# Splitting plain weight pieces two ahead instead of one in a Trainium2 macaron layer

## The chip, the cores and the metric

The kernel runs on one core of one Trainium2 chip. A core has engines that run side by side, each with its own queue in program order: TensorE (PE: matmuls into PSUM, and PEld: weight loads), VectorE (DVE), ScalarE (ACT), GpSimd (POOL, not used here) and SyncE (SP), whose queue issues the transfers from the chip's memory (DMA). The metric is device microseconds of one execution; shorter is better. The runs of the kernel before took 1015.99, 1016.55 and 1015.99 us (median 1015.99).

## The reference: what is computed

One layer on 512 tokens of width 1024: a half-weighted SwiGLU feed-forward, a mixer, a second half-weighted feed-forward, each behind an RMS norm and added to the residual, and a last norm.

```python
h = h + 0.5 * swiglu(rmsnorm(h, ffn1_norm[l]), ffn1_w_in[l], ffn1_w_out[l])
h = h + hybrid_mixer(rmsnorm(h, mix_norm[l]), w_mix_in[l], ...)
h = h + 0.5 * swiglu(rmsnorm(h, ffn2_norm[l]), ffn2_w_in[l], ffn2_w_out[l])

def swiglu(x, w_in, w_out):
    gate, up = jnp.split(x @ w_in, 2, axis=-1)
    return (jax.nn.silu(gate) * up) @ w_out
```

A feed-forward is 2816 wide (22 blocks of 128). The mixer projects to queries, keys and values of eight heads with compressed, selected and windowed attention and eight heads with a 128-token window, and ends in one more product, `w_mix_out`. All data are float32.

## The kernel before, in words

**Precision by parts.** TensorE takes the operands in a rounded 32-bit format. To keep float32 accuracy every operand is split: the high part is the rounded copy, the low part the rest, and a product is three matmuls, high x high, low x high, high x low (L207, L208, L209 for 512 tokens; L305, L306, L307 for 256). The normalized input is split once (`parts`, L162 on ACT and L163 on DVE). Weights are split piece by piece in `to_parts`: L97 is the ACT copy that makes the high part, L98 the DVE subtraction that makes the low part.

**The plain stream.** Weights that are used plainly come in pieces of 128 x 1024 in one stream: six pieces for the first three blocks (0, 1, 2) of each feed-forward (a gate piece and an up piece for each block), and the mixer's weights between them. `load_next` issues a piece's transfer, at most NRAW = 4 ahead; `split_next` takes the oldest loaded piece, splits it and loads another; `next_w` hands out the oldest split piece and splits one more, so that one split piece stands ready while one is used. A split piece takes two of the 32 buffers named `u`; a pair of raw pieces takes one of the four `t` buffers.

**A feed-forward's first blocks** (`ffn`, the loop `for j in range(plain)`). Each piece is one product `mm3` of eight contraction blocks, 24 matmuls. Beside them run the norm's sums: L170/L171 squares, `rstd_col` (L184 on PE, L186 and a table load on ACT, L188 on DVE) and `rstd_bc` (L195 on PE, L199 on ACT, into `bc`). Then each block's gated value: `gated` reads the gate product (L332, DVE), takes the silu (L334, ACT, behind a table load), reads the up product (L336), multiplies (L338), and splits the result (L325, L327).

**The side work** (`side_step`). The other 19 blocks use a form with seven products of quarter size in place of eight. It needs sums of the input, `sums_of_x`: eight scaled copies on ACT (L230), then per group differences on DVE (L238, L239, L242, L243) and splits (L246 on ACT, L247 on DVE); and sums of the weights, `sums_of_w`: L273, L277, L283 on DVE and splits (L275/L278, L281/L284, L287/L289, L292/L294). Block 3's first product needs the parts of L275 and L278. L483 sets two PSUM banks ahead of these products.

**The mixer's last product** is `mix_out((2, 3), True)`: two pieces, four output blocks from each; each output is added to the residual (L1077) and fed to the second feed-forward's norm.

**What sets the order.** The program is written in the order of the calls above, and a list scheduler with its own estimate of durations then orders each engine's queue. On the chip an engine takes its queue strictly in that order, and waits only where an instruction needs another engine's result or a free buffer.

Of the kernel before, what the change touches and what calls it, by code (L numbers as in the profile page):

```python
# [44 lines left out]
def tile_hybrid(ctx, tc, xT, f1_wi, f1_wo, wm_t, wm_n, cw1, cw2, small, wm_oa, wm_ob, wm_oc, f2_wi, f2_wo, const, out):  # L45
# [9 lines left out]
    def ps(tag="mm"):  # L55
        return psp.tile([P, 512], F32, tag=tag, name=tag, bufs=NB[tag])
# [4 lines left out]
    def ps_any():  # L61
        turn[0] += 1
        return ps(wide_ps[turn[0] % 5])

    def flat(dt=F32R):
        return sb.tile([P, 1024], dt, tag="u", name="u", bufs=NU)
# [25 lines left out]
    stream = []  # L92
    loaded, split = [], []
    half = []

    def to_parts(raw, wh, wl, c):
        A.copy(wh[:, c], raw[:, c])  # L97
        V.tensor_tensor(wl[:, c], raw[:, c], f(wh[:, c]), op=ALU.subtract)  # L98

    def raw_piece():  # L100
        if not half:
            t = double()
            half.extend([t[:, 0:1024], t[:, 1024:2048]])
        return half.pop(0)

    def load_next():
        if stream:
            src, n, whole = stream.pop(0)
            raw = raw_piece()
            nc.sync.dma_start(raw[:, :n], src)  # L110
            loaded.append((raw, n, whole))

    def split_next():
        if not loaded:
            load_next()
        if loaded:
            raw, n, whole = loaded.pop(0)
            if whole:
                split.append(raw)
            else:  # L120
                wh, wl = flat(), flat()
                to_parts(raw, wh, wl, slice(0, n))
                split.append((wh, wl))
            load_next()

    def load_ahead():
        while len(loaded) < NRAW and stream:
            load_next()

    def next_w():  # L130
        load_ahead()
        if not split:
            split_next()
        w = split.pop(0)
        split_next()
        return w

    def use(*pieces, n=1024, whole=False):
# [26 lines left out]
    def squares(k, acc):  # L165
        if k == 0:
            A.activation(acc, h[:, k, :], AF.Square)
        else:
            sq = tmp()
            A.activation(sq, h[:, k, :], AF.Square)  # L170
            V.tensor_tensor(acc, acc, sq, op=ALU.add)  # L171

    def feed(k, gcol, xs, acc):
        parts(k, gcol, xs)
        squares(k, acc)
# [4 lines left out]
    def rstd_col(acc):  # L180

        pc = ps("pv")
        for t in range(4):
            PE.matmul(pc[:, t : t + 1], acc[:, t * P : (t + 1) * P], ones[:, 0:1], start=True, stop=True)  # L184
        rc = sb.tile([P, 4], F32, tag="rc", name="rc", bufs=2)
        A.activation(rc, pc[:, 0:4], AF.Sqrt, scale=1.0 / D, bias=epsc[:, 0:1])  # L186
        rcol = sb.tile([P, 4], F32, tag="rcol", name="rcol", bufs=2)
        V.reciprocal(rcol, rc)  # L188
        return rcol

    def rstd_bc(rcol):

        pb = ps("pv")
        for t in range(4):
            PE.matmul(  # L195
                pb[:, t * P : (t + 1) * P], rcol[:, t : t + 1].to_broadcast([P, P]), ident, start=True, stop=True
            )
        bc = sb.tile([P, 512], F32, tag="bc", name="bc", bufs=1)
        A.copy(bc, pb)  # L199
        return bc  # L200

    def mm3_steps(o, wh, wl, ks, xs, first, last):
        for q, k in ks:
            c = slice(q * P, (q + 1) * P)
            s0 = first and k == ks[0][1]
            s1 = last and k == ks[-1][1]
            PE.matmul(o, wh[:, c], xs[k][:, 0, :], start=s0, stop=False)  # L207
            PE.matmul(o, wh[:, c], xs[k][:, 1, :], start=False, stop=False)  # L208
            PE.matmul(o, wl[:, c], xs[k][:, 0, :], start=False, stop=s1)  # L209
            yield 0.65  # L210

    def run(gen):
        for _ in gen:
            pass

    def mm3(*a):
        run(mm3_steps(*a))
# [36 lines left out]
    def load_raw(wi, j):  # L254
        t = double()
        for a in range(2):
            nc.sync.dma_start(t[:, a * 1024 : (a + 1) * 1024], wi[j, a])
        return t
# [50 lines left out]
    def ffn(xs, acc, wi, wo, plain, gnext):  # L309
# [20 lines left out]
        def gated(j, pg, pu):  # L330
            z = tmp()
            V.tensor_tensor(z, pg, bc, op=ALU.mult)  # L332
            sg = tmp()
            A.activation(sg, z, AF.Silu)  # L334
            zu = tmp()
            V.tensor_tensor(zu, pu, bc, op=ALU.mult)  # L336
            gg = tmp()
            V.tensor_tensor(gg, zu, sg, op=ALU.mult)  # L338
            run(put_g(j, gg))
# [86 lines left out]
        def side_step(n=1):  # L426
            for _ in range(n):
                while side and next(side[0], side) is side:
                    side.pop(0)
# [3 lines left out]
        for j in range(plain):  # L433
            pz = []
            if state["squares"] and j == 0:

                two = [(split.pop(0), ps_any()) for _ in range(2)]
                pz = [o for _, o in two]
                steps = [mm3_steps(o, wh, wl, ALLK, xs, True, True) for (wh, wl), o in two]
                for _ in ALLK:  # L440
                    for g in steps:
                        next(g, None)
                for g in steps:
                    run(g)
                split_next()
                for _ in range(4):
                    squares(*state["squares"].pop(0))
                side_step(4)
            for s in range(2 - len(pz)):
                wh, wl = next_w()  # L450
                o = ps_any()
                mm3(o, wh, wl, ALLK, xs, True, True)
                pz.append(o)
                if bc is None:
                    todo = state["squares"]
                    for _ in range(4):
                        if todo:
                            squares(*todo.pop(0))
                    if not todo and rcol is None:
                        rcol = rstd_col(acc)  # L460
                    elif rcol is not None:
                        bc = rstd_bc(rcol)
                        while held:
                            gated(*held.pop(0))
                side_step(4)
            if bc is None:
                held.append((j, *pz))
            else:
                gated(j, *pz)
            if j == 0:  # L470
                load_ahead()
                for n in range(2):
                    raws[plain + n] = load_raw(wi, plain + n)
                side.append(sums_of_w(raws, wi, plain, WF))
# [107 lines left out]
    for _ in range(2):  # L582
        src, _n, _whole = stream.pop(0)
        raw, wh, wl = raw_piece(), flat(), flat()
# [30 lines left out]
    for k in range(4, KB):  # L615
        parts(k, S_G1, xs)
    state["squares"] = [(k, acc) for k in range(KB)]
    xs, acc = ffn(xs, acc, f1_wi, f1_wo, NP1, S_GM)


# [38 lines left out]
    def proj(b, o):  # L659
        wh, wl = next_w()  # L660
        yield from mm3_steps(o, wh, wl, ALLK, xs, True, True)
# [29 lines left out]
    def network(kv):  # L691
# [5 lines left out]
        for c in range(2):  # L697
            oc = o[:, c * 64 : c * 64 + 62]
            for mh in range(2):
                w = next_w()  # L700
                for mm in range(8):
                    m = mh * 8 + mm
                    PE.matmul(  # L703
                        oc, w[:, mm * P : (mm + 1) * P], frv[:, mh, :, m : m + 241 : 8], start=m == 0, stop=m == 15
                    )
                    if mm % 4 == 3:
                        yield 0.86
            b1 = sm[:, S_B1 + kv * 2 + c : S_B1 + kv * 2 + c + 1]
            V.tensor_scalar(hT[:, c, :], oc, b1, None, op0=ALU.add)
# [358 lines left out]
    def mix_out(kbs, last):  # L1068
        n = len(kbs)
        per = KB // n  # L1070
        for c in range(KB // per):
            wh, wl = next_w()
            for j in range(per):
                i = c * per + j
                o = ps()
                yield from mm3_steps(o, wh, wl, [(j * n + q, kb) for q, kb in enumerate(kbs)], OB, True, True)
                V.tensor_tensor(h[:, i, :], o, h[:, i, :], op=ALU.add)  # L1077
                if last:
                    feed(i, S_G2, nxs, nacc)
# [78 lines left out]
    piece("q6", queries(6))  # L1158
    piece("q7", queries(7))
    piece("oa", mix_out((4, 5, 6, 7), False), [("s", 0, 3)])  # L1160
    piece("ob", mix_out((0, 1), False), [("n", 0, 3, 2)])
    nxs = []
    nacc = new_acc()
# [13 lines left out]
    while advance() is not None:  # L1177
        pass
    run(mix_out((2, 3), True))


    ffn(nxs, nacc, f2_wi, f2_wo, NP2, None)


# [90 lines left out]
```

## Time and profile before

| | |
|---|---|
| median of the runs | 1015.99 us |
| the profiled execution's own time | 1014.31 us |
| its span, first to last instruction | 1012.5 us |
| mean granted TensorE clock | 0.988 |
| PE busy | 982.1 us (97%) |
| PEld busy | 869.0 us (86%) |
| DVE busy | 804.2 us (79%) |
| ACT busy | 509.6 us (50%) |

A row of a timeline gives start, duration, engine, line, operation, output <- input and the count; in brackets the engine's idle time just before it and what ended it. A row of waits reads: who waited <- for whom: total us, times, longest. A row of windows is explained where it is shown. Granted clock is TensorE's, as a share of full speed. Names of buffers carry no meaning beyond the tile's name: `u` is a split operand, `t` a raw weight buffer, `sc`, `mm` and `pv` are PSUM tiles, `tmp` and `bc` vectors of 512 tokens.

### The profile page before, as it was taken

What the parts mean: (1) busy time and instruction counts of PE and PEld (TensorE: products, weight loads), DVE (VectorE), ACT (ScalarE), POOL (GpSimd) and SP (SyncE); (2) the same over time, 40 slices, a digit from 0 to 9 for tenths busy, and PEclk for the clock granted to TensorE, in tenths of its full rate; (3) what the DMA queues carried; (4) which work ended last, traced back from release to release, by engine and by line L of the source; (5) the groups of instructions that cost most, each with busy time, mean ns of one, the idle gap of its engine ahead of it and who ended that gap; (6) DMA issues with size and microseconds to landing.
All of it is one profiled execution on the core that took longest, in us unless ns stands there. A gap on an engine that the chain in (4) does not pass through costs nothing.

```text
span 1012.5 us, 15908 instructions
## 1 busy us (share of the span) xinstructions
PE 982.1 (97%) x6196; PEld 869.0 (86%) x6196; DVE 804.2 (79%) x1466; ACT 509.6 (50%) x1034; POOL 0.2 (0%) x4
## 2 busy tenths in 40 slices
PE   7799999999999999999999999989999999999997
PEld 5589999999999889788777777769999999999996
DVE  5889878788796675787889898788986878879665
ACT  7544434444344355554677675854434445344344
POOL 0000000000000000000000000000000000000000
PEclk9899999999999999999999999989999999999998
DMA  7053233222324303123311111115322323322112
GB/s 294 1 187 111 77 115 123 87 105 73 114 84 140 122 34 113 42 84 99 117 42 45 40 43 63 48 50 172 116 90 98 136 73 106 113 75 95 42 43 84
DMA packets 36508, 93.62 MB, mean 92 GB/s; under 512 B 4432, under 2 KB 8912, under 8 KB 36432
## 3 DMA queue, kind: packets, MB, share of 16 engines
q1 hardware_dynamic: 36432, 92.59, 26.8%
q8 instruction: 49, 0.80, 0.3%
q14 instruction: 27, 0.22, 0.1%
HBM read 88.87 MB, written 2.10 MB: 90 GB/s over the span
## 4 chain that ended last, share of the span: by engine, by line
PE 89%; DVE 6%; ACT 4%; issue 1%; DMA 1%; SPq 0%; DVEq 0%; ACTq 0%
PE mm L306 9%; PE mm L305 9%; PE mm L307 9%; PE sc L209 8%; PE sc L208 8%; PE sc L207 8%; PE mm L207 4%; PE mm L209 4%; PE mm L208 4%; PE sc L306 4%; PE sc L307 4%; PE sc L305 4%; PE mm L847 3%; PE pv L884 2%; PE pv L885 2%; PE mm L703 1%
## 5 line engine op out<-in xcount | busy, mean ns | idle before, releaser
L306 PE MATMUL mm<-u 128*128 128x256 f32 x760 | 214.5, 282 | 0.0
L307 PE MATMUL mm<-u 128*128 128x256 f32 x760 | 214.4, 283 | 0.0
L305 PE MATMUL mm<-u 128*128 128x256 f32 x760 | 214.3, 282 | 0.0
L207 PE MATMUL sc<-u 128*128 128x512 f32 (+1 forms) x400 | 156.5, 391 | 13.0 <-ACT u L97 12.0
L209 PE MATMUL sc<-u 128*128 128x512 f32 (+1 forms) x400 | 155.4, 388 | 0.8 <-DVE u L98 0.8
L208 PE MATMUL sc<-u 128*128 128x512 f32 (+1 forms) x400 | 155.8, 390 | 0.0
L305 PEld LDWEIGHTS mm<-u 128*128 128x128 f32 x760 | 144.5, 190 | 7.2 <-DVE tmp L512 0.5
L306 PEld LDWEIGHTS mm<-u 128*128 128x128 f32 x760 | 144.8, 191 | 5.6
L307 PEld LDWEIGHTS mm<-u 128*128 128x128 f32 x760 | 144.7, 191 | 0.6
L207 PE MATMUL mm<-u 128*128 128x512 f32 (+1 forms) x248 | 100.3, 404 | 4.6 <-ACT u L97 4.6
L209 PE MATMUL mm<-u 128*128 128x512 f32 (+1 forms) x248 | 96.6, 389 | 0.8 <-DVE u L98 0.8
L208 PE MATMUL mm<-u 128*128 128x512 f32 (+1 forms) x248 | 95.7, 386 | 0.6 <-DVE u L163 0.6
L207 PEld LDWEIGHTS sc<-u 128*128 128x128 f32 x400 | 77.3, 193 | 21.0 <-ACT u L97 12.9
L209 PEld LDWEIGHTS sc<-u 128*128 128x128 f32 x400 | 76.4, 191 | 20.4 <-DVE u L98 2.6
L307 PE MATMUL sc<-u 128*128 128x256 f32 x304 | 85.9, 283 | 0.0
L306 PE MATMUL sc<-u 128*128 128x256 f32 x304 | 85.9, 283 | 0.0
L305 PE MATMUL sc<-u 128*128 128x256 f32 x304 | 85.7, 282 | 0.0
L208 PEld LDWEIGHTS sc<-u 128*128 128x128 f32 x400 | 77.2, 193 | 6.5
L357 ACT CAST u<-tmp 128x512 fp32r<-128x512 f32 (+1 forms) x96 | 54.7, 583 | 45.4 <-PE sc L209 22.6
L380 DVE SCALAR_TENSOR_TENSOR h<-sc,h 128x512 f32<-128x512 f32 x85 | 58.3, 686 | 12.3 <-PE sc L209 12.3
L358 DVE TENSOR_TENSOR u<-tmp,u 128x512 fp32r<-128x512 f32 (+1 forms) x96 | 60.9, 640 | 8.9 <-ACT u L357 8.7
L493 ACT COPY mm<-sc 128x256 f32<-128x256 f32 x38 | 13.6, 357 | 94.7 <-PE sc L307 94.2
(221 smaller groups left out, 1994.4 us busy)
## 6 DMA issues: line engine op xcount, KB each, us to landing
t<-in_f_wi_dram SPq DMA_DIRECT2D x86, 512.0 KB, 4.4
tmp<-in_f_wo_dram SPq DMA_DIRECT2D x80, 256.0 KB, 4.7
t<-in_wm_t_dram SPq DMA_DIRECT2D x13, 512.0 KB, 4.4
t<-in_cw_dram SPq DMA_DIRECT2D x8, 512.0 KB, 4.9
tmp<-in_f_wo_dram SPq DMA_DIRECT2D x16, 128.0 KB, 4.0
t<-in_wm_oa_dram SPq DMA_DIRECT2D x4, 512.0 KB, 4.1
out_dram<-tmp SPq DMA_DIRECT2D x8, 256.0 KB, 2.1
t<-in_wm_n_dram SPq DMA_DIRECT2D x4, 408.0 KB, 3.7
```

The lines of the kernel that those rows point to most:

```text
L207: PE.matmul(o, wh[:, c], xs[k][:, 0, :], start=s0, stop=False)
L208: PE.matmul(o, wh[:, c], xs[k][:, 1, :], start=False, stop=False)
L209: PE.matmul(o, wl[:, c], xs[k][:, 0, :], start=False, stop=s1)
L305: PE.matmul(o, w[0][:, c], x[k][0], start=new, stop=False, skip_group_check=not first)
L306: PE.matmul(o, w[0][:, c], x[k][1], start=False, stop=False, skip_group_check=not first)
L307: PE.matmul(o, w[1][:, c], x[k][0], start=False, stop=k == 3, skip_group_check=not first)
L357: A.copy(u[:, 0, :n], raw[:, :n])
L358: V.tensor_tensor(u[:, 1, :n], raw[:, :n], f(u[:, 0, :n]), op=ALU.subtract)
L380: V.scalar_tensor_tensor(h[:, i, :], o, 0.5, h[:, i, :], op0=ALU.mult, op1=ALU.add)
L847: PE.transpose(pt[:rows, r * P : (r + 1) * P], pl[r][:, cols], ident)
L884: PE.matmul(pv, v, u[:rows, 0, :], start=a, stop=False)
L885: PE.matmul(pv, v, u[:rows, 1, :], start=False, stop=b)
```

## The change

`next_w` gets an argument: how many split pieces are to stand ready after one is handed out. It is 2 in the feed-forwards' first blocks and in the mixer's last product, and 1, as before, everywhere else. In the first feed-forward, where the first two pieces are taken together, two more are split behind them instead of one.

```diff
-    def next_w():
+    def next_w(ahead=1):
         load_ahead()
         if not split:
             split_next()
         w = split.pop(0)
-        split_next()
+        while len(split) < ahead and (loaded or stream):
+            split_next()
         return w
...
                 split_next()
+                split_next()
                 for _ in range(4):
                     squares(*state["squares"].pop(0))
...
             for s in range(2 - len(pz)):
-                wh, wl = next_w()
+                wh, wl = next_w(2)
                 o = ps_any()
                 mm3(o, wh, wl, ALLK, xs, True, True)
...
         for c in range(KB // per):
-            wh, wl = next_w()
+            wh, wl = next_w(2 if last else 1)
```

Lines behind the change have numbers one or two higher in the changed kernel (L230 becomes L231, L483 becomes L485).

What it moves. The ScalarE queue in the first feed-forward, before, from the split of piece 3. The raw pieces 3 and 4 lie in `t_169`, pieces 5 and 6 in `t_198`:

```order
L97 CAST u<-t_169 128x1024
L170 ACTIVATE tmp<-h 128x512
L230 ACTIVATE u<-h,sm 128x512 x8
L97 CAST u<-t_169 128x1024
L186 ACT_TABLE_LOAD
L186 ACTIVATE rc<-pv,epsc 128x4
L246 CAST u<-u 128x1024 x2
L199 COPY bc<-pv 128x512
L97 CAST u<-t_198 128x1024
L334 ACT_TABLE_LOAD
L334 ACTIVATE tmp<-tmp 128x512
```

Now, from the row behind the split of piece 3 (pieces 5 and 6 lie in `t_180`):

```order
L171 ACTIVATE tmp<-h 128x512
L97 CAST u<-t_169 128x1024
L231 ACTIVATE u<-h,sm 128x512 x8
L97 CAST u<-t_180 128x1024
L187 ACT_TABLE_LOAD
L187 ACTIVATE rc<-pv,epsc 128x4
L247 CAST u<-u 128x1024
L200 COPY bc<-pv 128x512
L247 CAST u<-u 128x1024
L335 ACT_TABLE_LOAD
L335 ACTIVATE tmp<-tmp 128x512
L97 CAST u<-t_180 128x1024
```

Piece 4's copy has moved from behind the eight input copies to ahead of them, piece 5's from behind both L246 to straight behind the eight, and piece 6's, eight rows behind these before, stands behind the first silu.

VectorE in the first feed-forward, now, from the row behind piece 6's low part and the L328 that follows it, to block 3's first low part (L279, L278 before):

```order
L239 TENSOR_TENSOR u<-u 128x512
L337 TENSOR_TENSOR tmp<-sc,bc 128x512
L240 TENSOR_TENSOR u<-u 128x512
L339 TENSOR_TENSOR tmp<-tmp 128x512
L333 TENSOR_TENSOR tmp<-mm,bc 128x512
L248 TENSOR_TENSOR u<-u 128x1024
L243 TENSOR_TENSOR u<-u 128x512
L244 TENSOR_TENSOR u<-u 128x512
L337 TENSOR_TENSOR tmp<-sc,bc 128x512
L339 TENSOR_TENSOR tmp<-tmp 128x512
L248 TENSOR_TENSOR u<-u 128x1024
L328 TENSOR_TENSOR u<-tmp,u 128x512
```

L279 is the next row. Before, piece 6's low part stood directly ahead of L278; now this work stands between them.

VectorE in the second feed-forward, before, from the read of piece 1's product to the low part of piece 4 (`t_6547`):

```order
L332 TENSOR_TENSOR tmp<-mm,bc 128x512
L239 TENSOR_TENSOR u<-u 128x512
L336 TENSOR_TENSOR tmp<-sc,bc 128x512
L338 TENSOR_TENSOR tmp<-tmp 128x512
L247 TENSOR_TENSOR u<-u 128x1024
L242 TENSOR_TENSOR u<-u 128x512
L243 TENSOR_TENSOR u<-u 128x512
L332 TENSOR_TENSOR tmp<-mm,bc 128x512
L247 TENSOR_TENSOR u<-u 128x1024
L327 TENSOR_TENSOR u<-tmp,u 128x512
L98 TENSOR_TENSOR u<-t_6547,u 128x1024
```

Now, from block 0's gated product to the low part of piece 5 (also in `t_6547`; piece 4's stands five rows ahead of this):

```order
L339 TENSOR_TENSOR tmp<-tmp 128x512
L333 TENSOR_TENSOR tmp<-mm,bc 128x512
L248 TENSOR_TENSOR u<-u 128x1024
L243 TENSOR_TENSOR u<-u 128x512
L244 TENSOR_TENSOR u<-u 128x512
L337 TENSOR_TENSOR tmp<-sc,bc 128x512
L339 TENSOR_TENSOR tmp<-tmp 128x512
L248 TENSOR_TENSOR u<-u 128x1024
L328 TENSOR_TENSOR u<-tmp,u 128x512
L98 TENSOR_TENSOR u<-t_6547,u 128x1024
```

The split at this place is now that of the piece after, and the read of piece 4's product (L337, L336 before) has moved ahead of piece 5's split. On ScalarE in the same way piece 6's copy stands directly behind the silu of piece 5's product (L335).

## The prediction

> Line numbers are those of the kernel before. "Piece 1" to "piece 6" are the six plain pieces of a feed-forward, two for each of blocks 0, 1 and 2; "block 3" is its first block in the seven-product form.
>
> **What bounds the kernel now.** I read the page first: the chain that ended last, then the costliest groups.
>
> ```profile
> PE 89%; DVE 6%; ACT 4%; issue 1%; DMA 1%; SPq 0%; DVEq 0%; ACTq 0%
> L207 PE MATMUL sc<-u 128*128 128x512 f32 (+1 forms) x400 | 156.5, 391 | 13.0 <-ACT u L97 12.0
> L207 PE MATMUL mm<-u 128*128 128x512 f32 (+1 forms) x248 | 100.3, 404 | 4.6 <-ACT u L97 4.6
> ```
>
> TensorE carries 89% of the chain, and the one release that costs it much is the high part of a weight piece (ACT, L97): 12.0 + 4.6 us. Next, busy time by window, to see where TensorE has no gap and how full VectorE is there. The columns are the window and its length, then PE, PEld, DVE, ACT and POOL busy (with instructions), the granted clock, DMA share and GB/s:
>
> ```profile
> 23.00:25.00 2.00, 2.00 (x10) 1.69 (x9) 0.82 (x1) 1.15 (x2) 0.00 (x0) 1.00 0.01 2
> 60.00:75.00 15.00, 15.00 (x104) 13.71 (x103) 13.66 (x24) 6.30 (x12) 0.00 (x0) 1.00 0.41 136
> 695.00:710.00 15.00, 15.00 (x107) 14.09 (x106) 14.47 (x26) 6.89 (x13) 0.00 (x0) 1.00 0.34 115
> ```
>
> Behind each feed-forward's plain blocks TensorE is full, so what is won ahead of 60 us is kept, if VectorE (13.66 of 15) follows. The same view of the first feed-forward, cut at the ends and starts of TensorE's work in the timeline:
>
> ```profile
> 33.39:36.74 3.35, 0.01 (x2) 0.00 (x1) 2.24 (x4) 2.51 (x4) 0.00 (x0) 0.85 0.00 0
> 36.74:42.65 5.91, 5.91 (x14) 4.61 (x15) 5.80 (x9) 3.70 (x5) 0.00 (x0) 0.51 0.00 1
> 42.65:45.40 2.75, 2.75 (x13) 2.06 (x11) 2.65 (x5) 0.48 (x1) 0.00 (x0) 1.00 0.00 0
> 45.40:48.91 3.51, 0.16 (x2) 0.01 (x1) 2.84 (x5) 3.09 (x5) 0.00 (x0) 1.00 0.00 0
> 48.91:52.85 3.94, 3.54 (x8) 2.44 (x9) 3.94 (x4) 3.31 (x4) 0.00 (x0) 0.57 0.35 111
> 52.85:56.49 3.64, 3.64 (x17) 3.00 (x16) 3.57 (x5) 0.00 (x0) 0.00 (x0) 1.00 0.78 244
> 56.49:59.37 2.88, 2.88 (x26) 2.87 (x25) 1.91 (x4) 1.24 (x3) 0.00 (x0) 1.00 1.03 399
> ```
>
> At full clock twelve 512-wide matmuls take 42.65 to 45.40, 0.227 each (a piece is 24 of them, 5.44 us); 24 of 256 take the last row's 2.88, 0.12 each. Piece 5 is waited for 3.35 us and piece 6 3.51. Behind each wait the clock is half: the 14 matmuls from 36.74 (12 wide, 2 narrow) are worth 2.96 and take 5.91, a loss of 2.95; the eight from 48.91 are worth 1.82 and take 3.94, a loss of 2.12. Together 11.9 us.
>
> The second feed-forward with the mixer's end ahead of it, and TensorE's waits from 600 to 695 us (total, times, longest):
>
> ```profile
> 640.35:647.72 7.37, 6.53 (x25) 4.08 (x23) 7.17 (x12) 5.11 (x9) 0.00 (x0) 1.00 0.44 142
> 647.72:654.30 6.58, 6.58 (x33) 5.51 (x33) 1.36 (x2) 6.55 (x11) 0.00 (x0) 1.00 0.00 0
> 654.30:661.52 7.22, 6.69 (x33) 5.16 (x31) 6.31 (x9) 4.29 (x5) 0.00 (x0) 1.00 0.43 145
> 661.52:664.99 3.47, 0.17 (x2) 0.01 (x1) 2.80 (x5) 3.03 (x4) 0.00 (x0) 0.82 0.00 0
> 664.99:670.65 5.66, 5.62 (x13) 3.96 (x13) 4.51 (x6) 1.04 (x1) 0.00 (x0) 0.50 0.01 3
> 670.65:679.72 9.07, 8.71 (x40) 7.05 (x38) 7.95 (x10) 4.65 (x6) 0.00 (x0) 1.00 0.00 0
> 679.72:688.64 8.92, 7.93 (x44) 6.75 (x42) 7.31 (x9) 3.17 (x5) 0.00 (x0) 1.00 0.68 229
> ```
>
> ```profile
> PE sc L207 <- ACT u L97: 3.3, 1, 3.3
> PE mm L207 <- ACT u L97: 1.0, 1, 1.0
> PE mm L209 <- DVE u L98: 0.8, 2, 0.5
> PE mm L208 <- DVE u L163: 0.6, 2, 0.3
> PE sc L209 <- DVE u L98: 0.4, 1, 0.4
> ```
>
> One long wait, 3.47 us, for piece 4, and 5.66 us at clock 0.50 for twelve matmuls worth 2.72, a loss of 2.94. Around it lie short waits, none of which costs the clock: piece 1 takes 7.37 us for 5.44, pieces 3 and 5 wait for a low part (L98), piece 6 waits 1.0; with the step lost beside each wait these last three are 0.7, 0.5 and 1.1.
>
> **The change part by part.** No instruction is added or removed. Each piece's ACT copy (L97) and DVE subtraction (L98) stand one place earlier, and the list scheduler has put the work around them anew. Durations for the walk:
>
> ```profile
> 18.20 5.01 ACT L230 ACTIVATE u<-h,sm 128x512 f32<-128x512 f32 x8
> 23.11 1.04 ACT L97 CAST u<-t 128x1024 fp32r<-128x1024 f32 x1
> 34.21 1.04 ACT L246 CAST u<-u 128x1024 fp32r<-128x1024 f32 x1 [2.62 <-DVE u L243]
> 35.16 0.58 ACT L199 COPY bc<-pv 128x512 f32<-128x512 f32 x1
> 35.64 1.05 ACT L97 CAST u<-t 128x1024 fp32r<-128x1024 f32 x1
> 36.70 1.28 ACT L334 ACT_TABLE_LOAD   x1
> 38.00 0.63 ACT L334 ACTIVATE tmp<-tmp 128x512 f32<-128x512 f32 x1
> 31.75 1.22 DVE L247 TENSOR_TENSOR u<-u 128x1024 fp32r<-128x1024 f32 x1
> 32.89 0.68 DVE L242 TENSOR_TENSOR u<-u 128x512 f32<-128x512 f32 x1
> 33.49 0.68 DVE L243 TENSOR_TENSOR u<-u 128x512 f32<-128x512 f32 x1
> 50.03 0.68 DVE L278 TENSOR_TENSOR u<-t,u 128x512 fp32r<-128x512 f32 x1
> ```
>
> In a full queue the next instruction starts some 0.09 us before such an end: DVE steps 1.14 (1024 wide) and 0.60 (512), ACT 0.95 and 0.53; the other engine starts 0.04 behind an end (33.49 + 0.68 to 34.21).
>
> *First feed-forward.* Piece 4's L97 now stands ahead of the eight L230, which run from 19.15 to 24.1 instead of 18.20 to 23.2; piece 5's L97 follows to 25.1, its L98 to 26.4. Its load has long landed (DMA share 0.01 from 23 us). TensorE gets to piece 5 at 33.39: **no wait, so 3.35 and the 2.95 behind it go.** Piece 5 ends at 38.83. Piece 6's L97 stands behind the second L246 (34.2 to 35.2), the table load (to 36.4) and the first silu (to 37.0), and ends at 37.97; its L98 starts at 38.27 behind L338 and L332 and ends at 39.49. TensorE wants that low part at 38.83 + 0.70 (two matmuls and the two of L483) = 39.53: no wait, by 0.04. Piece 6 ends at 44.5, not 56.49.
>
> What is late next is block 3's own split. VectorE has work almost without a gap from 28.6 on, and from piece 6's L98 to the low part of block 3's first weights (L278) the new order holds twelve instructions of 512 and two of 1024: 39.40 + 12 x 0.62 + 2 x 1.14 = 49.1 (0.62, as a few of them wait for the one before). TensorE can issue four narrow matmuls ahead of it. So it **stands from about 44.7 to 49.2** and then runs at half clock; I charge 2.5, between the 2.12 and 2.95 measured. The 24 matmuls of block 3's first two products end at 49.2 + 20 x 0.12 + 2.5 = 54.1 instead of 59.37. **Gain 5.3 us**; 7.8 if the clock stays full, 4.8 with the larger loss. Further on the splits keep a lead: block 4's L278 is eight DVE steps later, some 7 us, near 56, and TensorE wants it after four more products (48 x 0.12) and 18 wide matmuls (4.1), at 64. The loads of blocks 5 and 6 wait in SP's queue for these same splits, which come earlier. If VectorE did not follow, the gain would shrink to its own: L278 ended at 50.71, now at about 49.15, 1.6 us.
>
> *Mixer's last product.* Piece 1 is split there, behind piece 2 of the product itself, by an ACT that is nearly idle and a VectorE that waits for TensorE:
>
> ```profile
> 626.00:631.70 5.70, 5.70 (x27) 4.73 (x26) 4.61 (x8) 0.23 (x2) 0.00 (x0) 1.00 0.29 86
> 654.04 1.03 ACT L97 CAST u<-t 128x1024 fp32r<-128x1024 f32 x1
> 655.10 1.23 DVE L98 TENSOR_TENSOR u<-t,u 128x1024 fp32r<-128x1024 f32 x1 [5.04 <-ACT u L97]
> ```
>
> It costs nothing, at most the 1.14 of one L98 if that cover were gone. The 1.9 us that piece 1 loses (7.37 for 5.44) are mostly waits for the normalized input; the new order fills them with ten matmuls of piece 2, whose parts are there now. Piece 2 ends at 652.1, not 654.3; piece 3, its low part ready, ends at 658.4, not 661.5.
>
> *Second feed-forward.* The L97 at 654.04 and L98 at 655.10 are now piece 4's, ready at 656.3: no wait, it ends at 663.8 where it ended at 673.4. But VectorE's new order has the reads of piece 3's (L332) and piece 4's products (L336) *ahead* of piece 5's L98. VectorE is in order, so it stands until piece 4 is out at 664.0; then L336 and L338 (1.4), L247 (1.14), L327 (0.6) and L98 end at 668.4. TensorE issues two matmuls and stands: 4.6 us less 0.45. With 2.5 for half clock piece 5 ends at 668.4 + 22 x 0.227 + 2.5 = 675.9 (679.7 before). Piece 6 is placed worse: its L97 stands behind the silu of piece 5's product, 675.9 + 0.2 + 0.68 (L332) + 0.63 (silu) + 1.04 (L97) = 678.4, low part 679.6. Its 22 matmuls end at 684.6, ten of block 3 at 685.8, five more at 686.4; the same work ended at 688.5. **Gain 2.1.** If the stand of 2.5 us ahead of piece 6 also halves the clock, -0.8; if neither does, 4.6.
>
> **Sum**: 5.3 + 2.1 = 7.4. The profiled execution's own 1014.31 (span 1012.5) becomes 1006.9; the runs' median is 1015.99, 1.68 above it, so I forecast 1008.6.
>
> The trace has half clock behind 3.35, 3.51 and 3.47 us and full clock behind 1.0. [...]
>
> **The rivals.**
> - *Broken stands keep full clock.* For it: 1.0 us did. Against: both new stands last 4.5 us with only four narrow or two wide matmuls in them, and 3.35 was enough. 7.4 + 2.5 + 2.5 = 12.4: 1003.6.
> - *Piece 6 of the second feed-forward goes to half clock too* (2.5 us lies between the 1.0 and the 3.35 measured): 7.4 - 2.9 = 4.5: 1011.5. A missed margin of 0.04 at piece 6 of the first costs tenths and belongs here.
> - *No change.* VectorE, 91 and 96% full in the two windows above, does not follow, and TensorE gives its lead back: 1.6 at most from the first place, 0 from the second: 1014.4 or more. It needs the 8 us lead at block 4 to vanish. That the moved splits stay late because they wait for buffers belongs here too; in the new order they wait for their load alone.
> - *Slower.* The ring of the second feed-forward (product, VectorE's read, split, next product) closes one piece earlier, at piece 4. The point is 658.4: its split must come later than that, 2.1 us after what I computed. Then pieces 4, 5 and 6 each cost a stand and half clock, 3.47 + 2.94 = 6.4, together 19.2, against the 10.6 lost there now (1.9 at piece 1, 0.7 at piece 3, 3.5 and 2.9 at piece 4, 0.5 and 1.1 at pieces 5 and 6): 8.6 more, 5.3 won: 1019.3.
>
> **How the numbers follow.** Forecast 0.50; broken stands 0.14; second slow piece 0.20; no change 0.10; slower 0.06. The range that leaves out no more than 2 in 10 runs from near the first rival past the second: 1004.0 to 1013.0. A measurement of this kernel tells about 0.2% (2 us) from no change; the first three cases are faster by more, 0.84; the same 0.10; slower 0.06.
>
> **What would show it.** Right: no wait for pieces 5 and 6 near 33 and 39 us; one stand from about 44.7 to 49.2 ahead of block 3's first product, released by L275, L281 and L278, with clock 0.5 behind it; two more ahead of pieces 5 and 6 of the second feed-forward, released by an L98 behind a product's read and by an L97 behind a silu; TensorE full from 55 us on. Wrong: TensorE waiting for VectorE between 55 and 110 us, or piece 4 of the second feed-forward waiting for its split.

## The result, and the profile after

| | before | changed kernel |
|---|---|---|
| median of the runs, us | 1015.99 (1015.09 to 1017.62) | 1008.77 (1006.62 to 1010.84) |
| ratio of the times, 95% interval | | 0.9927 (0.991 to 0.9944) |
| profiled execution: time, span, us | 1014.31, 1012.5 | 1009.40, 1007.4 |

The changed kernel is 7.2 us faster (forecast: 1008.6, so 7.4). Its runs spread over 4.2 us, those of before over 2.5; two profiles of it show part of the reason (e5 below). In the changed kernel the lines from 136 on are shifted by one, those from 446 on by two: L207 is L208, L278 is L279, L703 is L705.

The chain of waits and the two costliest groups of the changed kernel's page:

```profile
PE 92%; DVE 4%; ACT 2%; DMA 1%; issue 1%; SPq 0%; DVEq 0%; ACTq 0%
L208 PE MATMUL sc<-u 128*128 128x512 f32 (+1 forms) x400 | 155.7, 389 | 7.5 <-ACT u L97 6.6
L208 PE MATMUL mm<-u 128*128 128x512 f32 (+1 forms) x248 | 99.0, 399 | 2.7 <-ACT u L97 2.7
```

TensorE's waits for the high part of a piece fall from 12.0 + 4.6 to 6.6 + 2.7 us, and 5.6 of the 6.6 is the first load of the kernel. The waits of its TensorE from 20 to 60 us, and then from 600 to 695:

```profile
PE sc L306 <- ACT u L276: 2.8, 1, 2.8
PE mm L306 <- ACT u L282: 0.4, 1, 0.4
PE sc L308 <- DVE u L279: 0.2, 1, 0.2
```

```profile
PE sc L210 <- DVE u L98: 2.7, 1, 2.7
PE mm L208 <- ACT u L97: 2.4, 1, 2.4
PE sc L208 <- ACT u L97: 1.0, 1, 1.0
```

No plain piece of the first feed-forward is waited for; block 3's own split is. In the second feed-forward piece 4 is not waited for, but piece 5 is, for both parts (1.0 and 2.7), and piece 6 (2.4). The same in busy time by window (columns as in the prediction), first the first feed-forward from piece 5's start, then the second from the end of piece 4:

```profile
33.67:39.68 6.01, 6.01 (x30) 4.96 (x28) 5.34 (x8) 5.60 (x7) 0.00 (x0) 1.00 0.00 1
39.68:45.44 5.76, 5.70 (x25) 4.24 (x23) 5.76 (x10) 1.69 (x2) 0.00 (x0) 1.00 0.70 248
45.44:48.21 2.77, 0.00 (x1) 0.01 (x1) 2.67 (x4) 2.14 (x4) 0.00 (x0) 1.00 0.15 52
48.21:49.82 1.61, 1.00 (x4) 0.59 (x4) 1.61 (x4) 1.61 (x2) 0.00 (x0) 1.00 0.00 0
49.82:53.46 3.64, 3.64 (x17) 3.64 (x18) 3.64 (x4) 2.42 (x5) 0.00 (x0) 0.53 0.01 2
```

```profile
661.10:665.58 4.48, 0.76 (x4) 0.30 (x3) 4.31 (x6) 0.99 (x2) 0.00 (x0) 0.87 0.00 0
665.58:673.48 7.90, 7.90 (x22) 5.96 (x22) 5.91 (x8) 2.09 (x2) 0.00 (x0) 0.64 0.00 0
673.48:675.92 2.44, 0.01 (x1) 0.00 (x0) 1.84 (x3) 1.61 (x3) 0.00 (x0) 1.00 0.00 0
675.92:681.40 5.48, 5.41 (x25) 4.40 (x26) 5.48 (x6) 3.85 (x5) 0.00 (x0) 1.00 0.49 187
```

What piece 5's low part stands behind on VectorE, and piece 6's high part on ScalarE (rows between are left out):

```profile
661.16 0.69 DVE L337 TENSOR_TENSOR tmp<-sc,bc 128x512 f32<-128x512 f32 x1 [1.62 <-PE sc L210]
...
664.30 1.22 DVE L98 TENSOR_TENSOR u<-t,u 128x1024 fp32r<-128x1024 f32 x1
...
674.31 0.63 ACT L335 ACTIVATE tmp<-tmp 128x512 f32<-128x512 f32 x1 [1.70 <-DVE tmp L333]
674.84 1.03 ACT L97 CAST u<-t 128x1024 fp32r<-128x1024 f32 x1
```

VectorE stands 1.62 us until piece 4's product is out, and the low part of piece 5 comes behind that read. This is the ring that the prediction speaks of: a product waits for a split, the split stands behind the read of an earlier product, and the read waits for that product.

To see where the gain lies I compare the same four instructions in both timelines: the first broadcast of the norm (ahead of piece 5), the last add into h of the first feed-forward, the last pair of adds of the mixer, and the last add into h of all. Before, then after:

```profile
32.34 1.05 PE L195 MATMUL pv<-ident,rcol 128*128 128x128 f32 x8
...
370.72 0.68 DVE L380 SCALAR_TENSOR_TENSOR h<-sc,h 128x512 f32<-128x512 f32 x1
...
643.61 1.29 DVE L1077 TENSOR_TENSOR h<-mm,h 128x512 f32<-128x512 f32 x2
...
1002.87 0.42 DVE L401 SCALAR_TENSOR_TENSOR h<-sc,h 128x256 f32<-128x256 f32 x1
```

```profile
32.86 1.05 PE L196 MATMUL pv<-ident,rcol 128*128 128x128 f32 x8
...
364.94 0.68 DVE L381 SCALAR_TENSOR_TENSOR h<-sc,h 128x512 f32<-128x512 f32 x1
...
640.63 1.28 DVE L1079 TENSOR_TENSOR h<-mm,h 128x512 f32<-128x512 f32 x2
...
998.21 0.42 DVE L402 SCALAR_TENSOR_TENSOR h<-sc,h 128x256 f32<-128x256 f32 x1
```

The stretches differ by +0.52 (the start, whose loads landed a little later: the 512 KB of h in 8.5 us against 7.7, medians), **-6.30** (first feed-forward), **+2.80** (mixer) and **-1.68** (second feed-forward); the final norm adds -0.5. The mixer's loss was not in the prediction. It is one event, at 471 us; the last column but two of the windows is the clock, and the two rows behind them are the DMA issues between 455 and 485 us, before first:

```profile
471.30:472.34 1.04, 0.00 (x1) 0.00 (x0) 0.94 (x5) 0.00 (x0) 0.00 (x0) 1.00 1.04 209
472.34:474.16 1.82, 1.82 (x13) 1.82 (x13) 0.10 (x1) 0.00 (x0) 0.00 (x0) 0.75 0.32 66
474.16:475.85 1.69, 1.69 (x9) 1.69 (x10) 0.00 (x0) 0.00 (x0) 0.00 (x0) 0.50 0.15 31
```

```profile
t<-in_cw_dram SPq DMA_DIRECT2D x1, 512.0 KB, 3.8
```

```profile
t<-in_cw_dram SPq DMA_DIRECT2D x1, 512.0 KB, 6.4
```

The load of one compression weight, issued at the same place of SP's queue, took 6.4 us instead of 3.8. TensorE waited 1.04 us for it and then ran at half clock.

### The profile page after: what moved, and what is told of

Its sections match the earlier page's. It is cut to its first block, busy times and chain, and to the rows that moved or that the text cites. A ratio compares the mean times of both kernels' runs of the same rounds, so it can differ in the third digit from the quotient of the medians.

```text
span 1007.4 us, 15922 instructions
## 1 busy us (share of the span) xinstructions
PE 979.0 (97%) x6196; PEld 869.4 (86%) x6196; DVE 802.1 (80%) x1466; ACT 509.7 (51%) x1034; POOL 0.2 (0%) x4
## 4 chain that ended last, share of the span: by engine, by line
PE 92%; DVE 4%; ACT 2%; DMA 1%; issue 1%; SPq 0%; DVEq 0%; ACTq 0%
PE mm L307 9%; PE mm L308 9%; PE mm L306 9%; PE sc L210 9%; PE sc L209 9%; PE sc L208 8%; PE mm L208 5%; PE mm L210 5%; PE mm L209 5%; PE sc L308 4%; PE sc L307 4%; PE sc L306 4%; PE mm L849 3%; PE pv L886 2%; PE pv L887 2%; PE sc L840 1%
## 5 line engine op out<-in xcount | busy, mean ns | idle before, releaser
L208 PE MATMUL sc<-u 128*128 128x512 f32 (+1 forms) x400 | 155.7, 389 | 7.5 <-ACT u L97 6.6
L209 PE MATMUL sc<-u 128*128 128x512 f32 (+1 forms) x400 | 155.5, 389 | 0.0
L208 PE MATMUL mm<-u 128*128 128x512 f32 (+1 forms) x248 | 99.0, 399 | 2.7 <-ACT u L97 2.7
L210 PE MATMUL mm<-u 128*128 128x512 f32 (+1 forms) x248 | 95.4, 385 | 0.3 <-DVE u L98 0.2
L209 PE MATMUL mm<-u 128*128 128x512 f32 (+1 forms) x248 | 94.8, 382 | 0.0
L210 PEld LDWEIGHTS sc<-u 128*128 128x128 f32 x400 | 76.2, 191 | 20.8 <-DVE u L98 3.6
L208 PEld LDWEIGHTS sc<-u 128*128 128x128 f32 x400 | 77.0, 193 | 15.3 <-ACT u L97 7.0
L209 PEld LDWEIGHTS sc<-u 128*128 128x128 f32 x400 | 77.0, 192 | 6.7 <-DVE u L164 0.3
L358 ACT CAST u<-tmp 128x512 fp32r<-128x512 f32 (+1 forms) x96 | 54.8, 583 | 45.3 <-PE sc L210 21.0
L306 PEld LDWEIGHTS sc<-u 128*128 128x128 f32 x304 | 58.2, 192 | 5.8 <-ACT u L276 3.2
```

Of the source, the lines that this page charges most:

```text
L306: PE.matmul(o, w[0][:, c], x[k][0], start=new, stop=False, skip_group_check=not first)
L358: A.copy(u[:, 0, :n], raw[:, :n])
```

## The experiments

All edits are against the changed kernel; the time of before in the same sessions was 1015.95 (e1 to e4), 1015.72 (e5 to e8) and 1015.37 (e9 to e11). The stretches of each profile are in one table behind the experiments.

### e1, e2: each place alone

```
-                wh, wl = next_w(2)                        # plain blocks
+                wh, wl = next_w(2 if gnext is not None else 1)
-            wh, wl = next_w(2 if last else 1)             # mixer
+            wh, wl = next_w()
```

> Only the first feed-forward splits two pieces ahead (its two pieces at the start of block 0 included); the mixer's last product and the second feed-forward split one ahead, as before. By the prediction's steps this part is worth 5.3 us: 1015.99 - 5.3 = 1010.7. By the trace of the changed kernel, read against that of before at the same instruction (the adds into h run 5.77 us earlier from 127 to 371 us, with a start that is 0.52 later), it is worth 6.3: 1009.7. Rival, a lead that VectorE gives back: 1014.4 or more. Rival, that the second place carries most of the 7.2 us measured: 1013 or more. In the profile the wait of 3.5 us for piece 4 of the second feed-forward should be back, with its half clock.

e2 is the reverse: `2 if gnext is None else 1` in the plain blocks, the mixer's line kept, and one `split_next()` at the start of block 0.

> Only the mixer's last product and the second feed-forward split two pieces ahead; the first feed-forward is that of before. By the prediction this part is worth 2.1 us: 1013.9. By the trace of the changed kernel (the lead shrinks to 2.97 us in the mixer and grows to 4.65 over this stretch) it is worth 1.7: 1014.3. If the ring of product, VectorE's read and next split eats all of it, 1016.0 or more; if it carries the larger part of the 7.2 us, 1011. The two waits of the first feed-forward, 3.35 and 3.51 us, should be back. If the wait for a compression weight in the mixer (1.04 us in the changed kernel's profile, none before) comes from the change, it should be absent or present here by the order alone; if it is chance of one transfer, it can be in any profile.

Measured: e1 1009.51 us, ratio 0.9943 (0.9931 to 0.9955); e2 1014.76, ratio 0.9986 (0.9977 to 0.9994). In e2 the two waits of the first feed-forward are back (4.4 and 3.3 us). The longest wait from 600 us on in e1 is piece 4's again:

```profile
PE sc L208 <- ACT u L97: 3.3, 1, 3.3
```

What follows: the first place is worth 6.4 us by the medians (6.28 in its profile), the second 1.2 (1.23 in its profile up to the last add); together 7.6 against the 7.2 of the whole, so nothing shows that the two touch each other. Both rivals, that the lead is given back and that the second place carries the gain, are out.

### e3: is the new stand a matter of order?

```
-                side.append(sums_of_w(raws, wi, plain, WF))
+                side.insert(0, sums_of_w(raws, wi, plain, WF))
```

> The changed kernel, with the sums and splits of block 3's weights queued ahead of the sums of the normalized input instead of behind them, in both feed-forwards. If the stand ahead of block 3 is set by the amount of VectorE's work (it has no gap from 28.6 us on, and the same steps must be done before the second product of block 3), the wait only moves, to piece 6's low part or to the first product that wants a sum of inputs: 1008.8 within 1.5 us. If it is set by the order alone, the stand of 4.1 us and the 1.9 us of half clock behind it go: 1002.8. In the second feed-forward piece 6's high part no longer stands behind a silu: if that place decides there, 2.4 us more.

Measured: 1010.30 us, ratio 0.9943 (0.9931 to 0.9956), 1.5 above the changed kernel, though the two intervals overlap. Three waits of its TensorE between 33 and 60 us, from the timeline (in brackets the idle time before and its releaser):

```profile
51.11 0.50 PE L306 MATMUL mm<-u 128*128 128x256 f32 x2 [2.75 <-ACT u L247]
52.37 0.42 PE L307 MATMUL mm<-u 128*128 128x256 f32 x1 [0.76 <-DVE u L248]
55.31 0.58 PE L306 MATMUL mm<-u 128*128 128x256 f32 x1 [0.59 <-DVE mm L505]
```

What follows: the stand only moved, from block 3's first weights to the sums of the input that its second product wants (L247, L248). It is VectorE's amount of work that sets it, as far as an order can tell. In the second feed-forward the wait for piece 6 is gone as well, and one of 2.6 us for another split (L358, of the output weights) has come in its place.

### e8, e9: less work for VectorE

```
-            V.tensor_tensor(u[:, 1, :], gg, f(u[:, 0, :]), op=ALU.subtract)
+            (nc.gpsimd if j < plain else V).tensor_tensor(u[:, 1, :], gg, f(u[:, 0, :]), op=ALU.subtract)
```

> The changed kernel, with the low part of each plain block's gated product computed on GpSimd, which is otherwise idle, instead of VectorE. That takes two of the fourteen VectorE instructions away that stand between piece 6's low part and block 3's first low part (0.62 us each), and one ahead of piece 5's low part in the second feed-forward; the order of the others stays. If VectorE's amount sets the stands, the one ahead of block 3 ends 1.24 us earlier and piece 5's 0.6: 1007.0, and up to 3.7 us less than the changed kernel's 1008.8 where a shorter stand no longer halves the clock. If something else releases them, 1008.8 (a late compression weight counts 2.8 in it or not). If GpSimd slows VectorE, it shows in the duration of VectorE's instructions of those stretches.

Measured: 1010.11 us, ratio 0.9942 (0.993 to 0.9955): no gain. GpSimd's and VectorE's instructions in e8's timeline, and then the same L279 in the changed kernel:

```profile
39.43 2.07 POOL L328 TENSOR_TENSOR u<-tmp,u 128x512 fp32r<-128x512 f32 x1 [38.99 <-ACT u L326]
48.47 1.99 POOL L328 TENSOR_TENSOR u<-tmp,u 128x512 fp32r<-128x512 f32 x1 [6.98 <-ACT u L326]
```

```profile
40.27 1.78 DVE L239 TENSOR_TENSOR u<-u 128x512 f32<-128x512 f32 x1
...
49.25 1.76 DVE L279 TENSOR_TENSOR u<-t,u 128x512 fp32r<-128x512 f32 x1
```

```profile
49.09 0.68 DVE L279 TENSOR_TENSOR u<-t,u 128x512 fp32r<-128x512 f32 x1
```

The two VectorE instructions beside those on GpSimd, L239 and L279, took 1.78 and 1.76 us, 1.1 more than the changed kernel's 0.69 and 0.68 and more than the 0.6 saved. So this test says nothing on the amount; e9 repeats it without GpSimd, with one profile. ScalarE writes `A.copy(u[:, 1, :], gg)` for the three plain blocks of the first feed-forward; the copy stands where the low part belongs, so these blocks' products count twice in what it computes.

> The changed kernel; in the first feed-forward the low parts of the three plain blocks' gated products are left out and ScalarE, which has room, writes a plain copy in their place. This leaves out part of the computation: the output loses these corrections. VectorE again has two instructions less (0.62 us each) ahead of block 3's first low part, this time with nothing on GpSimd. ScalarE has two copies more there, 0.53 each, one of them ahead of the high part of block 3's first weights. If VectorE's amount sets the stand, that low part ends near 48.7 us, 1.0 earlier than the 49.77 of the changed kernel (it then waits for ScalarE's high part, which ends near 48.1), and the third narrow matmul starts near 48.8 instead of 49.82. If VectorE's amount does not set it, it starts at 49.8 again. VectorE's instructions there should keep 0.68 us; the GpSimd run had them at 1.76 to 2.31.

Measured: 1010.22 us in its one run (before, in that session: 1015.37). e9's timeline:

```profile
48.83 0.69 DVE L279 TENSOR_TENSOR u<-t,u 128x512 fp32r<-128x512 f32 x1
```

Its start lies 0.72 later than the changed kernel's (the norm's broadcast at 33.58 against 32.86), so L279 comes 0.98 us earlier, as the amount theory said (1.0). Yet the first feed-forward gained 6.06 us in this profile, not 7.3: the clock behind the stand was half for two stretches of 3.41 us instead of one (the last section tells of them). The amount set where the stand ended; what the shorter stand was worth here was decided by the clock.

### e4, e6: filling the stands

```
+        if gnext is not None:
+            for _ in range(34):
+                PE.matmul(banks[0], xs[0][:, 0, :P], xs[0][:, 0, t1], start=True, stop=True)
```

> The changed kernel, with 34 more narrow matmuls (128 x 256, into a bank that block 3 writes anew before it is read) in the first feed-forward at the place of the two that are there already: four fall into piece 6, thirty, some 3.6 us, into the stand ahead of block 3. They compute nothing that is used. If the pace of 0.214 us per narrow matmul behind the stand is the halved clock that comes of the stand (20 matmuls took 4.3 us instead of 2.4), filling it gives those 1.9 us back, less 0 to 0.5 for the four in piece 6: 1006.9 to 1007.4. If the pace comes from something else (operands that arrive late), the added work gives nothing or costs its overhang: 1008.8 to 1009.8.

Measured: 1005.36 us, ratio 0.9899 (0.9886 to 0.9912). e4's timeline: thirty of the added matmuls fill the stand, the third narrow one of block 3 starts when VectorE is ready; then e4's window behind it:

```profile
45.04 3.75 PE L488 MATMUL mm<-u 128*128 128x256 f32 x30
...
49.46 0.39 PE L308 MATMUL sc<-u 128*128 128x256 f32 x1 [0.16 <-DVE u L279]
```

```profile
49.46:52.50 3.04, 3.04 (x25) 3.04 (x26) 3.04 (x3) 2.73 (x6) 0.00 (x0) 1.00 0.03 8
```

25 narrow matmuls in 3.04 us at full clock, where the changed kernel had 17 in 3.64 at 0.53. The first feed-forward takes 7.78 us less than before, 1.48 better than the changed kernel (expected 1.4 to 1.9). The medians differ by more, 3.4 (2.8 against e5 below), and 1005.36 is less than expected; what made the rest is open, as this variant has one profile and the changed kernel two.

e6 adds 24 matmuls ahead of piece 5 of the second feed-forward, into its own bank:

> The kernel with the filled stand ahead of block 3 (1005.36), and 24 further narrow matmuls, 2.9 us, ahead of piece 5 of the second feed-forward, into the bank that piece 5 then writes anew. They compute nothing that is used. That piece waits 1.02 us for its high part and 2.70 for its low part and then runs at 0.427 us for each of twelve wide matmuls, a loss of 2.4. If that is the clock and the stand its cause, 2.4 us come back: 1003.0. If the stand needs to be wholly empty to matter, or the pace has another cause, nothing changes: 1005.4. If VectorE or ScalarE wait for the added work somewhere, it gets slower than 1005.4 by up to 2.9.

Measured: 1006.74 us, ratio 0.9907 (0.9893 to 0.992). The 2.4 us expected did not come: it is 1.4 above e4, with overlapping intervals, and of the 1.75 between the two profiles 1.1 lie in the start, ahead of the edit. Piece 5, the wait for piece 6 and piece 6 in e6's windows:

```profile
662.06:667.33 5.27, 5.27 (x22) 4.05 (x22) 5.24 (x7) 1.05 (x1) 0.00 (x0) 1.00 0.00 0
667.33:670.61 3.28, 0.00 (x1) 0.00 (x1) 2.53 (x5) 2.56 (x4) 0.00 (x0) 0.91 0.00 0
670.61:676.00 5.39, 5.39 (x15) 4.42 (x16) 5.39 (x6) 3.83 (x5) 0.00 (x0) 0.50 0.56 190
```

Piece 5 keeps full clock (5.27 us, not 7.90), but piece 6 is then waited for 3.28 us instead of 2.44, and all of it runs at half clock. The stand is owed to the ring; won at one piece, it came back at the next.

### e5: the changed kernel again

> The changed kernel once more, not a word of it different. Its first profile holds a wait of 1.04 us in the mixer for a compression weight that took 6.4 us to land (3.8 in the profile of before, from the same place in the queue), and half clock behind it: the lead shrank there from 5.81 to 3.01 us. If that was chance of one transfer, this profile will most likely be without it and read 1006.6; if it belongs to the new order, it will be there again at 1009.4. The three profiles of the variants run so far have none of it, two of them with the new order of the first feed-forward.

Measured: 1008.17 us, ratio 0.9925 (0.9912 to 0.9937). The compression weight landed in 3.8 us and nothing waited for it; the mixer lost 0.14. The late load is chance, as the same kernel shows it once and once not: in the thirteen profiles it landed in 3.5 to 4.3 us nine times with no loss above 0.14, in 5.8 to 6.0 three times (e8, e10, e9) with 0.7 to 0.9 lost, and in 6.4 once with 2.8. But the profiled execution took 1008.79, not the 1006.6 expected, as the second feed-forward gained only 0.31 here. The wait for piece 6 and piece 6 in e5:

```profile
670.22:672.66 2.44, 0.00 (x0) 0.00 (x1) 1.84 (x3) 1.62 (x3) 0.00 (x0) 1.00 0.00 0
672.66:678.10 5.44, 5.38 (x17) 4.24 (x18) 5.44 (x6) 3.83 (x5) 0.00 (x0) 0.69 0.56 184
```

The same wait of 2.44 us, and now half clock behind it: 17 matmuls started in the 5.44 us in which the first profile has 25.

### e7, e10, e11: three pieces ahead

```
-                wh, wl = next_w(2)
+                wh, wl = next_w(2 if gnext is not None else 3)
```

e7 has it on top of e4's filled stand, e10 alone.

> The kernel with the filled stand ahead of block 3 (1005.36), the second feed-forward splitting three pieces ahead instead of two. The split of piece 5 then stands ahead of the reads of pieces 3 and 4, and piece 6's ahead of the silu that releases it now. If the ring of read, split and product is what holds pieces 5 and 6, their waits (1.02, 2.70 and 2.44 us) and the half clock (2.4) go, but the rest of VectorE's work is owed ahead of block 3, where a stand appears as it did in the first feed-forward. VectorE stood 1.6, 2.0 and 0.6 us between 652 and 682, so at most 4.2 us come from its side, and 2.4 if the clock stays: 998.8 at best, 1002 as a middle value. If the amount of VectorE's work holds them and not its order, 1005.4.

> The changed kernel with one number more changed: the second feed-forward splits three pieces ahead instead of two, with no filled stand. If the 5.5 us that this gave on top of the filled stand are its own, the changed kernel's 1008.2 to 1008.8 becomes 1002.7 to 1003.3. If it worked only together with the filled stand, 1008. The first feed-forward keeps its stand and one or two halves of 3.41 us at half clock behind it.

Measured: e7 **999.82 us**, ratio 0.9845 (0.9832 to 0.9859); e10 1003.63, ratio 0.9884 (0.9867 to 0.99). e7's waits from 600 to 695 us:

```profile
PE sc L308 <- DVE u L279: 1.6, 1, 1.6
PE mm L306 <- ACT u L282: 0.4, 1, 0.4
PE sc L306 <- ACT u L276: 0.2, 1, 0.2
```

The waits for pieces 5 and 6 are gone, and as in the first feed-forward block 3 is waited for instead, 2.2 us in all. The second feed-forward takes 7.10 us less than before, 6.0 better than e4's. The ring was what held it: with piece 5's split ahead of the reads of pieces 3 and 4, and piece 6's ahead of the read of piece 4, no split waits for a product. VectorE stands once for TensorE there, 1.37 us for piece 6's own product (L337, at 667.83), and L279, for which block 3 waits, comes behind it.

e11 fills both stands ahead of block 3, with matmuls that read piece 6's low part (`wl[:, :P]`) and so cannot start before it: `range(28 if gnext is not None else 14)`.

> Three ahead in the second feed-forward, and both stands ahead of block 3 filled with narrow matmuls that compute nothing used: 28 in the first feed-forward, 14 in the second. They read the low part of piece 6, so that none of them can fall into piece 6 (the four that did cost 0.48 us). In the profiles so far the clock changes only on a grid of 3.413 us, and in the feed-forwards a grid window in which TensorE was busy up to 1.68 us was followed by one at half clock, one with 1.70 or more by full clock. If that holds, no window at either stand falls under 1.7 now, the windows behind both are at full clock, and 0.5 + 1.5 us come off the 999.8 of the run with the first stand filled: 997.8. If the second stand is not worth filling, 999.3. Half clock behind either stand with its window over 1.7 us busy would refute the rule.

Measured: 999.22 us, ratio 0.9841 (0.9826 to 0.9855), no better than e7 within their spreads (998.96 to 1000.0 and 999.67 to 1001.05). The 997.8 expected was not reached. In its profile the second feed-forward is 0.5 better than e7's, where 1.5 was expected, and the clock is full at both stands; the second:

```profile
668.00:671.95 3.95, 2.90 (x22) 2.60 (x20) 3.17 (x5) 3.95 (x6) 0.00 (x0) 1.00 0.01 3
```

The 0.5 us expected from keeping the added matmuls out of piece 6 did not come (7.79 against 7.78): VectorE's chain ends the stand, and what TensorE does ahead of it is hidden. In e10's profile the clock stayed full at the second stand without any fill; there the fill could have won nothing.

The stretches of all profiles, in us against before (start: the norm's first broadcast; second feed-forward: up to the last add into h):

| | start | first ffn | mixer | second ffn |
|---|---|---|---|---|
| changed kernel | +0.52 | -6.30 | +2.80 | -1.68 |
| e5, the same again | +0.21 | -6.31 | +0.14 | -0.31 |
| e1 | +0.92 | -6.28 | +0.02 | +0.21 |
| e2 | +1.31 | +0.59 | +0.03 | -1.23 |
| e3 | -0.48 | -4.83 | +0.01 | -1.27 |
| e4 | +0.15 | -7.78 | +0.05 | -1.10 |
| e6 | +1.26 | -7.78 | -0.02 | -0.86 |
| e7 | +0.36 | -7.77 | +0.03 | -7.10 |
| e8 | +0.78 | -4.17 | +0.74 | -1.69 |
| e9 | +1.24 | -6.06 | +0.92 | -0.31 |
| e10 | +0.62 | -6.31 | +0.75 | -7.61 |
| e11 | +1.21 | -7.79 | +0.05 | -7.62 |

## Why the prediction was right, and where it was not

The total was right (1008.6 against 1008.77), the sum of its terms less so.

- **No wait at pieces 5 and 6 of the first feed-forward**: right but for tenths. Piece 6's margin of 0.04 us did not hold: its low part ended at 40.09 (38.87 + 1.22), and the matmul that reads it started at 40.14 instead of some 39.92, two steps of 0.12 behind the start of L485's pair at 39.68. The loss of 0.2 is the tenths that the second rival allows for.
- **The new stand, 44.7 to 49.2**: right. With the start 0.52 later it ran from 45.44 to 49.82, released by L276, L282 and L279; e3 and e9 show that VectorE's amount of work sets it.
- **Half clock behind it, charged 2.5**: too much. From 49.82 the remaining twenty matmuls of block 3's first two products took 4.0 us (to 53.82) instead of 2.4: 1.6. This is the step that made 6.3 out of 5.3; the bounds of 4.8 to 7.8 held it. The two figures that the charge lies between were not of one kind. The 2.12 holds 0.40 us in which TensorE was not busy (3.54 of 3.94), a wait for a low part (`PE sc L209 <- DVE u L98: 0.4, 1, 0.4`), so the clock cost 1.7 there, in one stretch at half clock (49.37 to 52.79). The 2.95 was two stretches (35.72 to 42.55). Block 3 had one (50.01 to 53.43).
- **VectorE follows**: right. TensorE waits for nothing from 54 to 121 us, and the lead is the same from 121 to 371 us. The rival "no change" is out.
- **The mixer costs nothing**: its moved split cost nothing (where the load was in time, the mixer's stretch differs by 0.14 us at most). But that the mixer has only some 1.6 us of margin against a late load (3.8 us to land, wanted after 5.4) was not seen: 2.8 us in the first profile, by chance.
- **Second feed-forward**: the walk was right to 0.6 us. Put back by the lead of 2.97 us that the profile has there, piece 5's low part ended at 668.5 (forecast 668.4), piece 5 at 676.5 (675.9) and piece 6's low part at 680.1 (679.6), by the queues named. Its size was not quite: half clock at piece 5 took 2.9 us (7.90 for 22 matmuls worth 4.99, over two stretches), where 2.5 was charged, and that 0.4 parts the 1.68 measured from 2.1. With piece 6 at full clock the stretch gained 1.68, and 1.23 in e2; with piece 6 at half clock 0.31 (e5).
- **The rivals**: that broken stands keep full clock is refuted by the two stands themselves (clock 0.53 and 0.64 behind them); e4 shows that the stand is the cause, since the fill alone brought the clock back (1.00 from 49.46 to 52.50). That piece 6 goes to half clock too, given 0.20, did happen in e4, e5, e8 and e9, and not in the first profile nor in e2. It differs from one execution of the same kernel to the next. The ring did not close at piece 4.

So the mechanism was right in both places, and the fit of the total to 0.2 us is in part luck. The profiled execution gained 4.9, not 7.4. The first feed-forward gave 1.0 more than forecast; the second gave 0.4 to 1.8 less in the two profiles of the kernel, and one of them has a late load. How much these last two take on average is not shown.

## What to carry to other kernels

When a split, a load or a read is moved one place ahead, walk the in-order queue of the engine that does it to the next consumer: the wait goes to whatever that engine now owes last, and its price is set by the engine's amount of work (first feed-forward) or by the ring that the order closes (second). If it is a ring, one place more may open it: three ahead instead of two was worth another 4.5 to 5.1 us alone (against 1008.17 and 1008.77, from other sessions) and 5.5 with the first stand filled. A stand of TensorE cost its own length here and then none, one or two stretches of 3.41 us at half clock (none at e10's second, one at the changed kernel's first, two at e9's first). With spare matmuls in the stand ahead of block 3 the clock stayed at 1.00 there in all four profiles that have them (e4, e6, e7, e11); where a ring makes the stand, filling it moved the stand to the next piece (e6), and opening the ring was what helped.

## What the runs showed of the hardware

**In these profiles the clock changed on a grid.** In each profile every change of the granted clock up to 692 us lies a whole number of 3.413 us from every other (before: down at 35.72, up at 42.55, down at 49.37, up at 52.79, down at 663.77, which is 628.05 us or 184.0 steps behind the first). The position of the grid differs from run to run (the changed kernel's first fall, at 50.01, lies 4.19 steps behind that of before). At half clock, grid windows (one step long) with up to 2.82 us busy (once 2.98) were followed by another one at half clock, and those with 2.93 or more by full clock: the changed kernel's stand ahead of piece 5, which reached 1.17 us beyond the edge at 664.41, cost two, and e8's ahead of block 3, which reached some 0.2 us into the next window (to 51.06), one. The piece 6 that behaved in two ways, in grid windows of the changed kernel and of e5 (the window with the stand, then the next):

```profile
674.65:678.06 3.41, 2.07 (x10) 1.65 (x11) 2.85 (x4) 3.41 (x5) 0.00 (x0) 1.00 0.00 0
```

```profile
670.97:674.39 3.42, 1.67 (x8) 1.33 (x9) 2.86 (x4) 3.35 (x5) 0.00 (x0) 1.00 0.00 0
674.39:677.80 3.41, 3.41 (x10) 2.66 (x9) 3.41 (x5) 2.10 (x3) 0.00 (x0) 0.50 0.82 267
```

In the changed kernel the grid cut the 2.44 us in two (671.24 to 674.65 has 2.25 us busy, this one 2.07) and the clock stayed; in e5 one window held nearly all of it (1.67 busy) and the next ran at 0.50. Over thirteen profiles, from 30 to 60 and 640 to 692 us, 26 of 27 windows ahead of a fall had 1.68 us busy or less, and of the windows at full clock that stayed there all but one had 1.69 or more. The two that do not fit are neighbours in e10 (1.54 busy and no fall, then 1.91 and a fall), so the edge is not sharp by the profile's busy time. All of this is for these matmuls of 256 and 512 columns: in the changed kernel's mixer, a window with 2.37 us busy (469.85 to 473.26), all of it 62-wide ones, was followed by half clock. One window at half clock costs up to 1.7 us by an estimate (half of 3.41); 1.6 was measured behind the changed kernel's first stand.

**VectorE took longer beside GpSimd (e8).** A subtraction of 128 x 512 with two inputs took 1.81 to 2.07 us on GpSimd in the first feed-forward and 1.27 to 1.32 in the second (0.68 on VectorE). The VectorE subtraction beside one of them (L279) took 1.76 us, where it took 0.68 in the changed kernel and 0.69 in e9, which have nothing on GpSimd; it ended at 51.01, 0.55 behind the one on GpSimd (50.46).

**A load of 512 KB, the compression weight's, issued from the same place, landed in 3.5 to 6.4 us** (3.8 before, 6.4 in the changed kernel's first profile). A consumer 5.4 us behind its issue was met nine times in thirteen with no loss above 0.14.
